# Convolution taps read from PSUM, and scan inputs fetched a step ahead, in a hybrid attention and state-space decoder step

## The chip, the cores and the metric

One core of one Trainium2 chip runs the whole program. The metric is the device time of one execution in microseconds (us). Five engines work side by side, each through its own instruction queue, in order: PE (TensorE, matmuls and transposes), DVE (VectorE), ACT (ScalarE), POOL (GpSimd) and SP (SyncE, which issues the DMAs here). PEld is PE's weight load. Results of PE land in PSUM, everything else is in SBUF or in device memory.

## The reference

One decoder layer for 1024 prompt tokens and 8 sample tokens. A norm feeds one wide projection `h @ w_in`, whose columns go to attention (q, k, v), to the state-space branch (z, xBC, dt) and to two gates. The change lies in the state-space branch:

```python
def _causal_conv(xbc, buf, w, bias):
    xp = jnp.concatenate([buf, xbc], axis=1)
    y = bias + xp[:, 0:L] * w[0]
    for t in range(1, D_CONV):          # D_CONV = 4
        y = y + xp[:, t:t + L] * w[t]
    return jax.nn.silu(y), xp[:, L:]
...
def _ssd(x, dt, A, Bm, Cm, h0):         # chunks of 128 tokens
    lmat = jnp.exp(_segsum(a))
    cb = jnp.einsum('bclgn,bcsgn->bcgls', Cc, Bc)
    y_diag = jnp.einsum('bcgels,bcsgep->bclgep', cb[:, :, :, None] * lmat, xf)
    decay_states = jnp.exp(a_cs[..., -1:] - a_cs)
    states = jnp.einsum('bclgn,bclgep->bcgepn', Bc, xf * decay_states[..., None])
    ...                                 # carry the states from chunk to chunk
    y_off = jnp.einsum('bclgn,bcgepn->bclgep', Cc, new_states[:, :-1]) * jnp.exp(a_cs)[...]
```

`xf` is x times dt. For the prompt `buf` is zero; for a sample token it is the stored window of three earlier tokens, and one step of the recurrence is done on a stored state. The convolution has 4096 channels: 2048 of x, 1024 of B, 1024 of C. There are 8 groups, each with 4 heads (256 channels of x) and 128 channels each of B and C.

## The kernel before

Features lie on partitions, tokens on columns. The 1032 tokens are cut into three chunks of 384, 384 and 264 columns (256 of the prompt and the 8 sample tokens). A `Dense` job computes 128 output features: for each chunk 24 matmuls (8 row tiles, three products of split weights and split inputs, L139 to L141) into one PSUM buffer `mm`, of which there are three, and then `evac` empties it. I call one such chunk a **dense step**. A weight tile comes by DMA (`wraw`), is rounded on ACT (`whi`, `shi`, L96), and POOL takes the rest (`wlo`, `slo`, L97).

The scan stage goes through the 8 groups. For group g the dense jobs are two of z (`z_jobs`, 6 steps) and then the four convolution jobs of group g+1 (`x_jobs`, 12 steps: two of x, one of B, one of C). Between the steps `pump` puts in **side work** of group g from three generators of `ssd_sides`: `chunks` (the scan over 8 chunks of 128 tokens: `prep`, `state`, `out`), `finish_` (norm, then `project`, eight tiles of output features of three chunks each, into the same `mm` buffers), and `decode` (the sample tokens). PE's order is the order in which the code runs; a scheduler sets the order of the other engines, which then work in that order.

What an `x_jobs` step does after its matmuls (L768 to L795): ACT copies PSUM to `rw`, a buffer of 387 columns of which there are two, whose first three columns are the last three of the chunk before (DVE, L775); ACT makes the fourth tap with the bias from PSUM into `acc` (a `ck` tile, L779); DVE adds the three earlier taps, reading `rw` (L781); for the sample tokens three small taps from `cvs` (L785); then tanh (ACT `th`, L789) and the product (DVE, L790). The last columns of a job are an output as well: `tail(i - 1)` is called in the first step of the next job, where PE transposes 11 columns of the `rw` of the step before (L801), and DVE copies them out (L802).

`prep(c)` (L860 to L889) starts the DMAs of the decay rows `ar` (256 KB, two buffers) and `er` where it uses them; ACT turns `ar` into exp(min(0, ...)) (L870, L872); PE transposes x and B and multiplies B with C into one PSUM tile; DVE masks that (`cb`) and makes `xd`; ACT copies `bt` and makes `xw` = `xd` times decay in four instructions (L887); POOL multiplies `ar` by `cb` (L888). `state` multiplies `xw` and `bt` (L894); `out` uses `ar` (L913). `decode` (L822 to L856) sends B and C of the sample tokens through memory (`bc_d`) and loads them broadcast (`bc`, one buffer) at the top of each of its four turns, with the states `hst` (two buffers).

Of the kernel before, what the change touches and what calls it, by code (L numbers as in the profile page):

```python
# [16 lines left out]
D = 1024  # L17
# [23 lines left out]
def _trunk(ctx, tc, nc, I, O):  # L41
# [16 lines left out]
    def h_tiles():  # L58
        return tuple([[hp_.tile([128, nt], F32R, name=p, tag=f"{p}{ci}", bufs=8) for ci, (_, nt) in enumerate(CH)]
                      for _ in range(8)] for p in ('hh', 'hl'))  # L60
# [22 lines left out]
    def load_w(src, r0, kt, c0, n, side=False, into=None, raw=None):  # L83
        """weights of kt row tiles by n columns, split into two float32r parts"""
# [15 lines left out]
    class Dense:  # L100
        """out^T[n features, tokens] for one tile of weight columns"""
        def __init__(self, src, r0, c0, n, x, evac, pre=None):
            self.a = (src, r0, c0, n, x, evac, pre)
            self.units = self.raw = None
# [19 lines left out]
        def steps(self):  # L124
            src, r0, c0, n, x, evac, pre = self.a
            if pre:
                pre()
            xh, xl = x if isinstance(x, tuple) else x()
            nk = len(xh)
            for ci, (t0, nt) in enumerate(CH):  # L130
                idle = 0
                while gated[0] and live[ci // 2] >= CKB[ci // 2] - 1 and idle < 20:
                    clock[0] += 1
                    idle = 0 if pump(2) else idle + 1
                ps = ps_mm()
                for k in range(nk):
                    wh, wl = self.units[k]
                    a, b = xh[k][ci], xl[k][ci]
                    T.matmul(ps[:n, :nt], wh, a, start=(k == 0), stop=False)  # L139
                    T.matmul(ps[:n, :nt], wh, b, start=False, stop=False)  # L140
                    T.matmul(ps[:n, :nt], wl, a, start=False, stop=(k == nk - 1))  # L141
                evac(ci, t0, nt, ps)
                yield
# [11 lines left out]
    def pump(n):  # L155
        """n slots of the side work; the oldest that need not wait come first"""
# [21 lines left out]
    def run(jobs, pace=0.0, after=None, ahead=1):  # L178
        """the dense jobs in order, with pace slots of side work after each step"""
# [40 lines left out]
    h_ = h_tiles()  # L220
    hh, hl = h_

    def rsqrt_cols(y, v, t):
        """y = v ** -0.5: a first guess from the exponent bits, then Newton steps"""
# [6 lines left out]
    class Mod:  # L231
        """512 of the modulation's columns; the weights move"""
# [48 lines left out]
    def rstd_cols(sq, scale, eps, pool):  # L281
        """(scale * column sums + eps) ** -0.5 of 384 columns, as [128, 3]"""
# [17 lines left out]
    with tc.tile_pool(name="p0", bufs=1) as p0:  # L300
# [55 lines left out]
        def make_h(ci):  # L356
# [12 lines left out]
            for k in range(8):  # L369
# [9 lines left out]
                V.tensor_copy(hh[k][ci], h[:, :nt])  # L379
                (P if k % 2 else V).tensor_tensor(hl[k][ci], h[:, :nt], hh[k][ci], op=OP.subtract)  # L380

# [40 lines left out]
    def attn_jobs(u, tiles):  # L422
        """q, k, v of two heads: the prompt's tokens ordered by residue, then the sample tokens"""
# [29 lines left out]
    def attn_side(u, tiles):  # L453
# [22 lines left out]
        def tok(j):  # L476
            # token-major k (where it is an output) and v
# [69 lines left out]
        for j in range(11):  # L547
# [3 lines left out]
            if j == 0:  # L551
                # rows of the sample tokens
# [100 lines left out]
    def dt_side(dp):  # L653
# [46 lines left out]
        A.activation(df, df, AF.Exp)  # L700
        A.activation(cdk.rearrange("p c h -> p (c h)"), p2[:, :256], AF.Exp)
# [11 lines left out]
        # sample: dt, exp(dt A) and D per (head, channel) partition  # L713
# [37 lines left out]
    def x_jobs(gi, tl):  # L751
# [3 lines left out]
        def post():  # L755
            for lo, n, i0, i1 in ((chans[0], 256, 0, 2), (chans[2], 128, 2, 3), (chans[3], 128, 3, 4)):
                src = st['t'][:, i0:i1, :].rearrange("r a b -> r (a b)")
                dma(cpr[:, lo:lo + n], src[0:3])
                dma(dap(O['conv_sample'], 2 * 4096 + lo, [[3 * 4096, 8], [1, n]]), src[3:11])

        jobs = []
        for i, ch in enumerate(chans):
            f = ch // 128
            prev = []
            tl['x'].append([None] * 3)

            def evac(ci, t0, nt, ps, i=i, f=f, prev=prev):
# [15 lines left out]
                if nt > n:  # L783
                    for k in range(3):
                        V.scalar_tensor_tensor(acc[:, n:nt], cvs[:, f, k, :], w[k], acc[:, n:nt],  # L785
                                               op0=OP.mult, op1=OP.add)
                    tl['tail'].append((i, rw, n, nt))
# [5 lines left out]
                if ci == 0 and i > 0:  # L793
                    tail(i - 1)

            def tail(i):
                _, rw, n, nt = tl['tail'][i]
                if i == 0:
                    st['t'] = sa.tile([24, 4, 128], F32, name="tail", tag="tail", bufs=1)
                pt = ps_()  # L800
                T.transpose(pt[:11, :128], rw[:, n:3 + nt], ident)  # L801
                V.tensor_copy(st['t'][:11, i, :], pt[:11, :128])  # L802

            if i == 3:
                def fin(tail=tail):
                    tail(3)
                    post()
                tl['fin'] = fin
            col = (X_C + gi * 256 + i * 128) if i < 2 else ((B_C if i == 2 else C_C) + gi * 128)
            jobs.append(Dense(w_in, 0, col, 128, h_, evac))  # L810
        return jobs

    def ssd_sides(gi, tl):
# [8 lines left out]
        def decode():  # L822
# [5 lines left out]
            rb = sd.tile([8, 2, 128], F32, name="rb", tag="rb", bufs=1)  # L828
# [4 lines left out]
            dma(bc_d[gi].rearrange("k b n -> b k n"), rb)  # L833
            yield from rest(2)
            for bh in range(4):
                bc = sd.tile([128, 2, 2, 128], F32, name="bc", tag="bc", bufs=1)
                dma(bc, dap(bc_d, gi * 2048 + bh * 256, [[0, 128], [1024, 2], [128, 2], [1, 128]]))
                for t in range(2):
                    r0 = bh * 2 * 262144 + (4 * gi + 2 * t) * 8192
                    hst = sd.tile([128, 2, 128], F32, name="hst", tag="hst", bufs=2)  # L840
                    dma(hst, dap(ws, r0, [[128, 128], [262144, 2], [1, 128]]))
# [4 lines left out]
                    tmp = sd.tile([128, 2, 128], F32, name="tmp", tag="tmp", bufs=1)  # L846
                    for i in range(2):
                        A.mul(tmp[:, i, :], bc[:, 0, i, :], dx[:, i:i + 1])
                        V.scalar_tensor_tensor(hst[:, i, :], hst[:, i, :], ds[:, 8 + 2 * bh + i:9 + 2 * bh + i],
                                               tmp[:, i, :], op0=OP.mult, op1=OP.add)  # L850
# [662 lines left out]
```

## Time and profile before

| what | value |
|---|---|
| three timed runs | 2601.06, 2606.17, 2608.93 us (median 2606.17) |
| profiled execution, span | 2599.9 us (the page gives no other time for it) |
| PE busy | 2413.3 us, 93% of the span |
| PE weight loads | 2278.0 us, 88% |
| DVE, ACT, POOL busy | 1409.6, 976.0, 827.7 us (54%, 38%, 32%) |
| scan stage | about 470 to 1480 us |

Matmuls are pipelined, so that a busy PE is not a PE at its peak. The span lies 6.3 us under the median of the timed runs. In the chain of work that ended last PE has 30% of the span, DVE 2%, and nothing else over 1%. The stage of the last projections (1900 to 2500 us) shows PE busy without a gap; the scan stage does not.

### The profile page before, as it was taken

The numbers are of one execution on the slowest core, as the hardware profiler recorded it, in microseconds if no ns is written. First come the engines' busy times: TensorE is split into PE (matmuls) and PEld (weight loads), VectorE is DVE, ScalarE is ACT, GpSimd is POOL, SyncE is SP. The second block draws the span as 40 slices with busy tenths as digits, with TensorE's granted clock in tenths as the row PEclk, the third lists the DMA queues.
The fourth block names the chain that finished last, engine by engine and source line by source line (L and its number), as shares of the span: only waits on it lengthen the run. The fifth ranks groups of instructions, "written<-read, shape, count | busy, mean of one in ns | idle before, by whom it ended". The sixth has DMA issues, their size and how long they took to land. (4 is left out here: it accounts for less than half of the span.)

```text
span 2599.9 us, 42044 instructions
## 1 busy us (share of the span) xinstructions
PE 2413.3 (93%) x15342; PEld 2278.0 (88%) x15342; DVE 1409.6 (54%) x3738; ACT 976.0 (38%) x2476; POOL 827.7 (32%) x759
## 2 busy tenths in 40 slices
PE   6999999988989898989898999889999999999998
PEld 3788888978888888889888898879999999999997
DVE  7634334586777777777778533553733333333336
ACT  6244443454535353535353422242412212221222
POOL 5322222243434343434343333353222122222230
PEclk8999999999999999999999999999999999999999
DMA  6433334243233333333333223332145444511111
GB/s 221 124 89 108 107 92 114 78 107 94 73 88 75 87 73 85 78 82 78 84 80 82 76 64 85 96 117 65 54 164 168 138 154 144 173 45 50 57 41 66
DMA packets 341944, 250.59 MB, mean 96 GB/s; under 512 B 22750, under 2 KB 324393, under 8 KB 339034
## 3 DMA queue, kind: packets, MB, share of 16 engines
q1 hardware_dynamic: 341738, 247.91, 33.4%
q8 instruction: 121, 1.98, 0.3%
q14 instruction: 85, 0.70, 0.1%
HBM read 224.50 MB, written 67.58 MB: 112 GB/s over the span
## 5 line engine op out<-in xcount | busy, mean ns | idle before, releaser
L139 PE MATMUL mm<-hh,whi 128*128 128x384 f32 (+2 forms) x2856 | 939.3, 329 | 2.9 <-ACT whi L96 2.0
L140 PE MATMUL mm<-hl,whi 128*128 128x384 f32 (+2 forms) x2856 | 919.9, 322 | 4.2 <-POOL hl L380 3.6
L141 PE MATMUL mm<-hh,wlo 128*128 128x384 f32 (+2 forms) x2856 | 918.9, 322 | 1.3 <-POOL wlo L97 1.3
L97 POOL TENSOR_TENSOR wlo<-wraw,whi 128x512 fp32r<-128x512 f32 (+2 forms) x304 | 399.0, 1319 | 863.7 <-ACT whi L96 800.0
L139 PEld LDWEIGHTS mm<-hh,whi 128*128 128x128 f32 (+1 forms) x2856 | 546.0, 191 | 12.0 <-issue 3.2
L140 PEld LDWEIGHTS mm<-hl,whi 128*128 128x128 f32 (+1 forms) x2856 | 545.8, 191 | 9.8 <-POOL hl L380 5.9
L141 PEld LDWEIGHTS mm<-hh,wlo 128*128 128x128 f32 (+1 forms) x2856 | 544.4, 191 | 2.7 <-POOL wlo L97 1.7
L96 ACT CAST whi<-wraw 128x512 fp32r<-128x512 f32 (+2 forms) x304 | 182.8, 611 | 358.5 <-PE mm L140 314.3
L1190 DVE SCALAR_TENSOR_TENSOR acc<-mm,mod,acc 128x384 f32<-128x384 f32 (+1 forms) x216 | 123.5, 572 | 244.9 <-PE mm L141 244.9
L140 PE MATMUL mm<-dl,whi 128*128 128x384 f32 (+1 forms) x696 | 223.2, 321 | 0.0
L141 PE MATMUL mm<-dh,wlo 128*128 128x384 f32 (+1 forms) x696 | 222.4, 320 | 0.0
L139 PE MATMUL mm<-dh,whi 128*128 128x384 f32 (+1 forms) x696 | 222.3, 319 | 0.0
L781 DVE SCALAR_TENSOR_TENSOR ck<-rw,cwT,ck 128x384 f32<-128x384 f32 (+1 forms) x288 | 193.1, 671 | 9.2 <-ACT ck L779 7.1
L1303 DVE TENSOR_TENSOR r<-r 128x384 f32<-128x384 f32 (+1 forms) x96 | 69.5, 724 | 185.6 <-ACT r L1302 185.4
L888 POOL TENSOR_TENSOR ar<-ar,cb 128x512 f32<-128x512 f32 x64 | 81.9, 1281 | 245.9 <-ACT ar L872 223.3
L969 PE MATMUL mm<-ck,shi 128*128 128x384 f32 (+1 forms) x384 | 131.2, 342 | 28.2 <-DVE acc L975 13.2
L971 PE MATMUL mm<-ck,slo 128*128 128x384 f32 (+1 forms) x384 | 128.2, 334 | 5.4 <-POOL slo L97 5.4
L139 PEld LDWEIGHTS mm<-dh,whi 128*128 128x128 f32 x696 | 131.1, 188 | 0.0
L140 PEld LDWEIGHTS mm<-dl,whi 128*128 128x128 f32 x696 | 131.0, 188 | 0.0
L141 PEld LDWEIGHTS mm<-dh,wlo 128*128 128x128 f32 x696 | 130.8, 188 | 0.0
L970 PE MATMUL mm<-ck,shi 128*128 128x384 f32 (+1 forms) x384 | 127.5, 332 | 1.3 <-POOL ck L952 1.3
L870 ACT ACTIVATE ar<-ar,acs 128x128 f32<-128x128 f32 x256 | 84.2, 390 | 104.9 <-DMA ar<-ac_d 101.7
(337 smaller groups left out, 3776.4 us busy)
## 6 DMA issues: line engine op xcount, KB each, us to landing
wraw<-w_in SPq DMA_DIRECT2D x164, 256.0 KB
kv_g_sample<-cache_kv_g SPq DMA_DIRECT2D x144, 256.0 KB
wraw<-w_ada SPq DMA_DIRECT2D x96, 256.0 KB
ar<-ac_d SPq DMA_DIRECT2D x64, 256.0 KB
wraw<-w_up SPq DMA_DIRECT2D x64, 256.0 KB
wraw<-w_down SPq DMA_DIRECT2D x58, 256.0 KB
hst<-state_ssm SPq DMA_DIRECT2D x64, 128.0 KB
bc<-bc_d SPq DMA_DIRECT2D x32, 256.0 KB
```

What stands on the lines that cost most here:

```text
L96: A.copy(hi, raw)
L97: P.tensor_tensor(lo, raw, hi, op=OP.subtract)
L139: T.matmul(ps[:n, :nt], wh, a, start=(k == 0), stop=False)
L140: T.matmul(ps[:n, :nt], wh, b, start=False, stop=False)
L141: T.matmul(ps[:n, :nt], wl, a, start=False, stop=(k == nk - 1))
L781: V.scalar_tensor_tensor(acc[:, :n], rw[:, k:k + n], w[k], acc[:, :n], op0=OP.mult, op1=OP.add)
L870: A.activation(ar[:, h, :], ar[:, h, :], AF.Relu, bias=acs[:, c, 4 * gi + h:4 * gi + h + 1], scale=-1.0)
L888: P.tensor_tensor(ar, ar, cb[:, None, :].to_broadcast([128, 4, 128]), op=OP.mult)
L969: T.matmul(ps[:, :nt], hi[:, t, :], a, start=(t == 0), stop=False)
L970: T.matmul(ps[:, :nt], hi[:, t, :], b, start=False, stop=False)
L971: T.matmul(ps[:, :nt], lo[:, t, :], a, start=False, stop=(t == 1))
L1190: V.scalar_tensor_tensor(x[:, t0:t0 + n], ps[:, :n], gate[:, 0:1], x[:, t0:t0 + n], op0=OP.mult, op1=OP.add)
```

## The change

- The inputs `hh` and `hl` of chunks 1 and 2 are laid out with four more columns in front (`HALO`), which repeat the last four tokens of the chunk before. 32 small ACT copies fill them in the stage of the first norm (behind L380 of the kernel before). The four convolution jobs of each group use these wider inputs, so that their PSUM buffer holds the tokens that the taps need; all other jobs use the slices without them.
- `rw`, the PSUM copy and the 3-column copy go. The three taps on DVE read PSUM, with `acc` from SBUF. For the sample tokens bias and three earlier taps are added up once at the stage's start (`conv_side`), and one small instruction per job is left. ACT copies the 11 last columns of each job to `last`, and `fin` transposes all four jobs' columns in one place.
- `ar` is fetched by `load` three chunks ahead (three buffers); `bc` and `hst` one turn ahead (two and three buffers); `tmp` has three small buffers in place of one large.
- `xw` is made by one DVE instruction from PSUM with dt and decay multiplied beforehand, in place of four on ACT; `cb` comes after it and has one buffer; the ACT work on `ar` comes after these in the code.
- The rounded copy `hi_` in `norm` moves from DVE to ACT.

```diff
+                m = nt + (self.halo if ci else 0)
                 for k in range(nk):
                     wh, wl = self.units[k]
                     a, b = xh[k][ci], xl[k][ci]
-                    T.matmul(ps[:n, :nt], wh, a, start=(k == 0), stop=False)
+                    T.matmul(ps[:n, :m], wh, a, start=(k == 0), stop=False)
...
+                if ci:
+                    for x, y in zip(hx_, h_):
+                        A.copy(x[k][ci][:, :HALO], y[k][ci - 1][:, CH[ci - 1][1] - HALO:])
...
+        V.tensor_tensor(dcy, dcy, dtk[:, :8], op=OP.mult)
...
+        def fin():
+
+            pt = ps_()
+            for i in range(4):
+                T.transpose(pt[:11, i * 128:(i + 1) * 128], st['last'][:, i, :], ident)
+            for p, parts in enumerate((((chans[0], 0, 256),), ((chans[2], 0, 128), (chans[3], 128, 128)))):
+                t = sa.tile([11, 256], F32, name="tail", tag="tail", bufs=2)
+                A.copy(t, pt[:11, p * 256:(p + 1) * 256])
...
-            def evac(ci, t0, nt, ps, i=i, f=f, prev=prev):
+            def evac(ci, t0, nt, ps, i=i, f=f):
...
-                rw = sa.tile([128, 387], F32, name="rw", tag="rw", bufs=2)
-                if ci == 0:
-                    V.memset(rw[:, 0:3], 0.0)
-                else:
-                    V.tensor_copy(rw[:, 0:3], prev[-1][:, 384:387])
-                prev.append(rw)
-                A.copy(rw[:, 3:3 + nt], ps[:, :nt])
+                x0 = HALO if ci else 0
                 acc = ck(nt, 1)
-                A.activation(acc[:, :nt], ps[:, :nt], AF.Identity, bias=bias, scale=w[3])
+                A.activation(acc[:, :n], ps[:, x0:x0 + n], AF.Identity, bias=bias, scale=w[3])
                 for k in range(3):
-                    V.scalar_tensor_tensor(acc[:, :n], rw[:, k:k + n], w[k], acc[:, :n],
+                    d = 3 - k
+                    o = 0 if ci else d
+                    V.scalar_tensor_tensor(acc[:, o:n], ps[:, x0 + o - d:x0 + n - d], w[k], acc[:, o:n],
                                            op0=OP.mult, op1=OP.add)
                 if nt > n:
...
+                    A.copy(st['last'][:, i, :], ps[:, x0 + n - 3:x0 + nt])
...
-                if ci == 0 and i > 0:
-                    tail(i - 1)
...
-            jobs.append(Dense(w_in, 0, col, 128, h_, evac))
+            jobs.append(Dense(w_in, 0, col, 128, hx_, evac, halo=HALO))
...
+            load(0)
             yield from rest(2)
             for bh in range(4):
-                bc = sd.tile([128, 2, 2, 128], F32, name="bc", tag="bc", bufs=1)
-                dma(bc, dap(bc_d, gi * 2048 + bh * 256, [[0, 128], [1024, 2], [128, 2], [1, 128]]))
...
+                load(bh + 1)
+                bc, hs_ = got[bh]
...
+        def load(c):
+
+            if c > 7:
+                return
+            ar = D_[c] = sd.tile([128, 4, 128], F32, name="ar", tag="ar", bufs=3)
+            dma(ar, dap(ac_d, 4 * gi * 1024 + c * 128, [[0, 128], [1024, 4], [1, 128]]))
...
         def prep(c):
-            ar = sd.tile([128, 4, 128], F32, name="ar", tag="ar", bufs=2)
-            dma(ar, dap(ac_d, 4 * gi * 1024 + c * 128, [[0, 128], [1024, 4], [1, 128]]))
+            ar = D_.pop(c)
...
             A.copy(bt, pt[:, 256:384])
+            V.tensor_tensor(xw, pt[:, :256].rearrange("p (h d) -> p h d", h=4),
+                            dcy[:, c, hs, None].to_broadcast([128, 4, 64]), op=OP.mult)
+            V.tensor_tensor(cb, pt[:, 384:512], tri, op=OP.mult)
             for h in range(4):
-                A.mul(xw[:, h, :], xd[:, h, :], dcy[:, c, 4 * gi + h:4 * gi + h + 1])
...
-                V.tensor_copy(hi_[t, ci], y)
+                A.copy(hi_[t, ci], y)
...
                 if c + 2 < 8:
                     prep(c + 2)
+                load(c + 3)
```

On PE, in the convolution of the sixth group, behind the first step of the last job, before (`L801` is the transpose of `rw`, `L944` one of the norm's; the next dense step begins behind it):

```order
L140 MATMUL mm<-hl,whi 128x384
L141 MATMUL mm<-hh,wlo 128x384
L801 MATMUL ps<-cst,rw 11x128
L944 MATMUL ps<-cst,rstd 128x128 x3
L139 MATMUL mm<-hh,whi 128x384
```

And now, in the same place:

```order
L142 MATMUL mm<-hh,whi 128x384
L143 MATMUL mm<-hl,whi 128x384
L144 MATMUL mm<-hh,wlo 128x384
L960 MATMUL ps<-cst,rstd 128x128 x3
L142 MATMUL mm<-hh,whi 128x388
```

The transpose has left the convolution's steps. Four of them stand together in the next group's first step of z, behind the transposes of `prep`, where the fourth job's stood before.

On ACT, from the second to the third step of the third convolution job of that group, before (`rw` is the copy of PSUM, `ck<-mm` the fourth tap, `th` the tanh):

```order
L789 ACTIVATE th<-ck 128x384
L777 COPY rw<-mm 128x384
L779 ACTIVATE ck<-mm,vecT,cwT 128x384
L932 ACTIVATE sq<-ck 128x264
L96 CAST whi<-wraw 128x512 x2
L789 ACTIVATE th<-ck 128x384
L777 COPY rw<-mm 128x264
L779 ACTIVATE ck<-mm,vecT,cwT 128x264
L96 CAST shi<-wraw 128x256
L789 ACTIVATE th<-ck 128x264
```

And now:

```order
L801 ACTIVATE th<-ck 128x384
L788 ACTIVATE ck<-mm,vecT,cwT 128x384
L948 ACTIVATE sq<-ck 128x264
L97 CAST whi<-wraw 128x512 x2
L801 ACTIVATE th<-ck 128x384
L788 ACTIVATE ck<-mm,vecT,cwT 128x256
L799 COPY last<-mm 128x11
L801 ACTIVATE th<-ck 128x264
L97 CAST shi<-wraw 128x256
```

The copies of PSUM are gone and the small `last` copy stands in front of the tanh of its step; the tanh of one step still stands ahead of the fourth tap of the next.

On SP, the DMAs behind the store of B and C of the sample tokens in that stage, before (`bc` is their broadcast load, `wraw` weights):

```order
L833 DMA bc_d<-rb 8x2x128
L80 DMA wraw<-w_o_ssd 128x2x128
L837 DMA bc<-bc_d 128x2x256
L80 DMA wraw<-w_o_ssd 128x2x128
L862 DMA ar<-ac_d 128x4x128
L853 DMA ssm_sample<-hst 128x2x128
```

And now:

```order
L829 DMA bc_d<-rb 8x2x128
L81 DMA wraw<-w_o_ssd 128x2x128
L836 DMA bc<-bc_d 128x2x256 x2
L875 DMA ar<-ac_d 128x4x128
L81 DMA wraw<-w_o_ssd 128x2x128 x2
L861 DMA ssm_sample<-hst 128x2x128
```

The second turn's `bc` moved up behind the first; the first still stands close behind the store that it reads.

## Rows read from the trace of the kernel before

**Rows 1.** Stretches: us; busy us (count) of PE, PEld, DVE, ACT, POOL; clock; DMA; GB/s

```profile
470.00:1480.00 1010.00, 906.46 (x5876) 859.92 (x5876) 739.63 (x2067) 472.76 (x1323) 378.53 (x360) 0.96 0.33 83
1900.00:2500.00 600.00, 600.00 (x3827) 600.00 (x3826) 203.76 (x431) 131.76 (x258) 137.91 (x107) 1.00 0.35 112
```

**Rows 2.** Waits of PE in 470 to 1480 us: total us, times, longest us

```profile
PE ps L801 <- ACT rw L777: 40.5, 15, 4.7
PE ps L894 <- ACT xw L887: 21.2, 13, 3.5
PE mm L969 <- ACT shi L96: 12.5, 6, 2.6
PE mm L969 <- DVE acc L975: 11.1, 9, 2.2
PE mm L971 <- POOL slo L97: 5.4, 6, 0.9
```

**Rows 3.** PE's timeline in the sixth group: start us, us, instruction, [idle before <-releaser]

```profile
1101.61 0.34 PE L141 MATMUL mm<-hh,wlo 128*128 128x384 f32 x1
...
1114.38 0.39 PE L801 MATMUL ps<-cst,rw 128*11 128x128 f32 x1 [4.67 <-ACT rw L777]
```

**Rows 4.** ACT's timeline in the same steps

```profile
1071.28 0.40 ACT L870 ACTIVATE ar<-ar,acs 128x128 f32<-128x128 f32 x1 [4.85 <-DMA ar<-ac_d]
...
1087.08 0.99 ACT L870 ACTIVATE ar<-ar,acs 128x128 f32<-128x128 f32 x3 [3.53 <-DMA ar<-ac_d]
...
1113.53 0.52 ACT L789 ACTIVATE th<-ck 128x384 f32<-128x384 f32 x1 [3.67 <-DVE rstd L227]
1113.96 0.36 ACT L777 COPY rw<-mm 128x264 f32<-128x264 f32 x1
```

**Rows 5.** DVE's timeline just before that

```profile
1108.88 0.16 DVE L229 SCALAR_TENSOR_TENSOR rstd<-rstd 128x3 f32<-128x3 f32 x1
...
1109.69 1.22 DVE L228 SCALAR_TENSOR_TENSOR rstd<-rstd 128x3 f32<-128x3 f32 x1
...
1111.18 1.61 DVE L781 SCALAR_TENSOR_TENSOR ck<-rw,cwT,ck 128x384 f32<-128x384 f32 x1
...
1112.82 0.62 DVE L781 SCALAR_TENSOR_TENSOR ck<-rw,cwT,ck 128x384 f32<-128x384 f32 x1
```

**Rows 6.** POOL's timeline at the same time

```profile
1109.48 2.89 POOL L97 TENSOR_TENSOR wlo<-wraw,whi 128x512 fp32r<-128x512 f32 x2 [7.88 <-DMA conv_sample<-tail]
```

**Rows 7.** Waits of ACT in 470 to 1480 us

```profile
ACT ar L870 <- DMA ar<-ac_d: 101.7, 40, 5.3
ACT tmp L848 <- DMA bc<-bc_d: 87.3, 27, 5.8
```

**Rows 8.** Groups by form in 470 to 1480 us: count | busy us, mean ns | idle before

```profile
L139 PE MATMUL mm<-hh,whi 128*128 128x384 f32 x753 | 266.7, 354 | 0.0
...
L781 DVE SCALAR_TENSOR_TENSOR ck<-rw,cwT,ck 128x384 f32<-128x384 f32 x179 | 133.5, 746 | 6.6 <-ACT ck L779 4.5
...
L139 PE MATMUL mm<-hh,whi 128*128 128x264 f32 x376 | 110.5, 294 | 0.0
...
L887 ACT ACTIVATE xw<-xd,dcy 128x64 f32<-128x64 f32 x256 | 71.4, 338 | 0.0
...
L781 DVE SCALAR_TENSOR_TENSOR ck<-rw,cwT,ck 128x256 f32<-128x256 f32 x90 | 48.8, 542 | 2.0 <-ACT ck L779 2.0
...
L883 DVE TENSOR_TENSOR xd<-ps,dtk 128x256 f32<-128x256 f32 x64 | 26.2, 410 | 0.0
...
L775 DVE COPY rw<-rw 128x3 f32<-128x3 f32 x59 | 21.9, 371 | 25.4 <-ACT rw L777 25.3
```

**Rows 9.** Min/median/max ns of the taps (470 to 1480) and L1190 (1900 to 2500)

```profile
L781 DVE SCALAR_TENSOR_TENSOR ck<-rw,cwT,ck x269: 462/605/1676, 469.8 to 1393.3; 128x384 f32<-128x384 f32 x90, 128x256 f32<-128x256 f32 x45
L1190 DVE SCALAR_TENSOR_TENSOR acc<-mm,mod,acc x168: 482/617/621, 1902.8 to 2488.2; 128x384 f32<-128x384 f32 x112, 128x256 f32<-128x256 f32 x56
```

**Rows 10.** The stage in which the halo is filled, as rows 1

```profile
70.00:80.00 10.00, 7.98 (x48) 4.88 (x48) 8.64 (x30) 4.80 (x9) 4.80 (x6) 0.98 0.01 2
```

More of the change, by code (lines that the diff above doesn't have):

```diff
@@ L56, in ps_, with h_tiles @@
         return psum.tile([128, 512], F32, name="ps", tag="ps", bufs=5)
-    def h_tiles():
-        return tuple([[hp_.tile([128, nt], F32R, name=p, tag=f"{p}{ci}", bufs=8) for ci, (_, nt) in enumerate(CH)]
-                      for _ in range(8)] for p in ('hh', 'hl'))
+    def h_tiles(halo=0):
+        return tuple([[hp_.tile([128, nt + (halo if ci else 0)], F32R, name=p, tag=f"{p}{ci}", bufs=8)
+                       for ci, (_, nt) in enumerate(CH)] for _ in range(8)] for p in ('hh', 'hl'))
     def chs(t):
@@ L218, in _trunk @@
     ac_d = dram.tile([2, 32, 1024], F32, name="ac_d")
-    h_ = h_tiles()
-    hh, hl = h_
+    HALO = 4
+    hx_ = h_tiles(HALO)
+    hh, hl = hx_
+    h_ = tuple([[t[:, HALO if ci else 0:] for ci, t in enumerate(r)] for r in x] for x in hx_)
     def rsqrt_cols(y, v, t):
@@ L833, in decode, with load @@
             dma(bc_d[gi].rearrange("k b n -> b k n"), rb)
+            got = {}
+            def load(bh):
+                if bh > 3:
+                    return
+                bc = sd.tile([128, 2, 2, 128], F32, name="bc", tag="bc", bufs=2)
+                dma(bc, dap(bc_d, gi * 2048 + bh * 256, [[0, 128], [1024, 2], [128, 2], [1, 128]]))
+                hs_ = []
+                for t in range(2):
+                    r0 = bh * 2 * 262144 + (4 * gi + 2 * t) * 8192
+                    hst = sd.tile([128, 2, 128], F32, name="hst", tag="hst", bufs=3)
+                    dma(hst, dap(ws, r0, [[128, 128], [262144, 2], [1, 128]]))
+                    hs_.append((r0, hst))
+                got[bh] = bc, hs_
+            load(0)
             yield from rest(2)
             for bh in range(4):
-                bc = sd.tile([128, 2, 2, 128], F32, name="bc", tag="bc", bufs=1)
-                dma(bc, dap(bc_d, gi * 2048 + bh * 256, [[0, 128], [1024, 2], [128, 2], [1, 128]]))
[L838 to L841, printed above, removed]
+                load(bh + 1)
+                bc, hs_ = got[bh]
+                for t, (r0, hst) in enumerate(hs_):
                     ds = dsel[:, 2 * gi + t, :]
@@ L845, in decode @@
                     V.tensor_tensor(dx[:, :2], xcol, ds[:, 2 * bh:2 * bh + 2], op=OP.mult)
-                    tmp = sd.tile([128, 2, 128], F32, name="tmp", tag="tmp", bufs=1)
                     for i in range(2):
-                        A.mul(tmp[:, i, :], bc[:, 0, i, :], dx[:, i:i + 1])
+                        tmp = sd.tile([128, 128], F32, name="tmp", tag="tmp", bufs=3)
+                        A.mul(tmp, bc[:, 0, i, :], dx[:, i:i + 1])
                         V.scalar_tensor_tensor(hst[:, i, :], hst[:, i, :], ds[:, 8 + 2 * bh + i:9 + 2 * bh + i],
-                                               tmp[:, i, :], op0=OP.mult, op1=OP.add)
-                        V.tensor_tensor_reduce(tmp[:, i, :], hst[:, i, :], bc[:, 1, i, :], 1.0, 0.0,
+                                               tmp, op0=OP.mult, op1=OP.add)
+                        V.tensor_tensor_reduce(tmp, hst[:, i, :], bc[:, 1, i, :], 1.0, 0.0,
                                                OP.mult, OP.add, dx[:, 4 + i:5 + i])
@@ L980, in chunks @@
         def chunks():
+            while gi and tls[gi - 1]['c'] < 8:
+                yield 'wait'
+            for c in range(3):
+                load(c)
             while tl['nx'] < 12:
@@ L1028, in finish @@
             assert idle < 50
-    tls = [dict(z=[], x=[], tail=[], nz=0, nx=0, c=0, dec=0) for _ in range(8)]
+    tls = [dict(z=[], x=[], nz=0, nx=0, c=0, dec=0) for _ in range(8)]
     atl = [[] for _ in range(6)]
@@ L1055, in _trunk @@
     sa = sa_cm.__enter__()
-    cvs = sa.tile([128, 32, 3, 8], F32, name="cvs")
+    cvs = sa.tile([128, 32, 8], F32, name="cvs")
     def conv_side():
@@ L1072, in conv_side @@
                             ident[:24, :24])
-            V.tensor_copy(cvs[:, f0:f0 + 16], ps[:, :384].rearrange("p (i b k) -> p i k b", i=16, k=3))
+            pv = ps[:, :384].rearrange("p (i b k) -> p i k b", i=16, k=3)
+            fs = slice(f0, f0 + 16)
+            c, t = (sa.tile([128, 384], F32, name="th", tag="th", bufs=2)[:, :128]
+                    .rearrange("p (i b) -> p i b", i=16) for _ in range(2))
+            for k in range(3):
+                V.tensor_tensor(t if k else c, pv[:, :, k, :], cwT[:, k, fs, None].to_broadcast([128, 16, 8]),
+                                op=OP.mult)
+                if k:
+                    V.tensor_tensor(c, c, t, op=OP.add)
+            V.tensor_tensor(cvs[:, fs], c, vecT[:, R_CB + f0:R_CB + f0 + 16, None].to_broadcast([128, 16, 8]),
+                            op=OP.add)
             yield
```

55 lines of the change are left out of this document (21 added, 34 removed).

## The prediction

> **What bounds the kernel now.** I first read the busy time by stretch. From 1900 to 2500 us PE is busy for 600.0 of 600 us at a granted clock of 1.00; from 470 to 1480 us, the scan stage, for 906 of 1010 at a mean clock of 0.96 [rows 1]. The stages differ in what ends the waits, so I then read PE's own waits in the scan stage [rows 2], and from the longest of them back to its cause [rows 3 to 6]. The other engines are not full there (DVE 740 us, ACT 473, POOL 379 of 1010, [rows 1]); what counts is how late they are, since each works its queue in order.
>
> The longest wait of PE is that of the small transpose L801 for the copy `rw`: 40.5 us in 15 places [rows 2]. One of them: PE stands for 4.67 us up to 1114.38, so from 1109.71, since ACT makes `rw` only at 1113.96 [rows 3, 4]. ACT stood 3.67 us in front of a tanh, for the taps that end on DVE at 1113.4 [rows 4, 5]. And DVE was late for two reasons. ACT had itself stood 4.85 and 3.53 us in this group for a DMA of the decay rows [rows 4]; and two of DVE's instructions took 1.22 and 1.61 us in place of some 0.16 and 0.61, while POOL worked on two weight tiles [rows 5, 6]. Over the stage ACT stood 101.7 us for the decay rows and 87.3 us for `bc` [rows 7].
>
> [...]
>
> **The change part by part**, against the profiled execution, whose span is 2599.9 us; the median of the timed runs is 6.3 us above it.
>
> *The transposes of `rw`.* All of the 40.5 us go, because no transpose stands in the convolution any more. The four that stand together later take the place of the fourth job's, 8 in all; where the fourth job's transposes did not wait, and the `last` copies are in ACT's queue ahead of the tanh. −40.5 (bounds −24, if the eight waited 2 us each, and −40.5).
>
> *`xw`.* PE waits 21.2 us in 13 places for ACT's four `xw` instructions [rows 2], which take 4 x 0.338 us behind the four on `ar` and their exponent [rows 8]. One DVE instruction takes their place; its nearest row is `xd` from the same PSUM tile, 410 ns [rows 8]. It needs no decay rows. `bt` remains on ACT. −17 (bounds −10 and −21).
>
> *Prefetch.* `project` waits 12.5 us for ACT's `shi`, 5.4 us for POOL's `slo` that follows it, and 11.1 us for DVE's `acc` [rows 2], 29 in all. ACT's queue holds `tmp` and `ar` ahead of `shi`, and stands on their DMAs [rows 7]; DVE's `hst` stands on `tmp`. A chunk's decay rows are now issued one chunk earlier, some 6 us, where the worst wait was 5.3 us [rows 7]; so that wait should all but vanish. `bc` of turns 2 to 4 comes a turn earlier, but that of turn 1 still stands close behind the store that it reads, so one of four of these waits remains. I take 60%: −17.5 (bounds 0 and −29).
>
> *The clock.* 75 of the 91 us of PE's waits above go. I take 60% of the 40 us: −24 (bounds 0 and −40).
>
> *The halo's columns.* 32 jobs x 2 chunks x 24 matmuls = 1536 matmuls with 4 more columns. A matmul of 384 columns has a mean of 354 ns, one of 264 of 294 ns [rows 8]: 0.5 ns a column, 2.0 ns for four, +3.1 us. All of it lies on PE.
>
> *The halo's copies.* 32 on ACT, each at most the 338 ns of an instruction with 64 columns [rows 8], 11 us at most. In that stage ACT is busy for 4.8 of 10 us and PE for 8.0 [rows 10], so most lies in ACT's idle time. +2 (bounds 0 and +11).
>
> *The taps, and who holds PSUM.* Before, an `mm` buffer came free with the copy and the fourth tap, both on ACT. Now it is held until the third tap is done on DVE (and, in the last chunk, the `last` copy), and the step three later waits for that. Behind a waiting step on PE stands all of PE's work. An instruction of that form (PSUM times a column, plus SBUF) is L1190: 482 and 617 ns for 256 and 384 columns, with a maximum of 621. The taps from `rw` have a median of 605 but a maximum of 1676 [rows 9] and means of 746 and 542 [rows 8]. So 179 taps become 129 ns shorter and 90 become 60 ns shorter: −28 us on DVE. The copies of 3 columns (21.9 us [rows 8]) go as well; `xw` brings 64 x 0.410 = 26 us. DVE is a little lighter by that alone, ACT by the 71 us of `xw` [rows 8] and the copies. How late are the taps now? In the example the taps that end at 1113.4 are those of the step that ended at 1101.95 [rows 3], 11.5 us earlier. The step three later would have started at about 1110, just behind 1109.71, so that PE would have stood 3.4 us for PSUM in place of 4.67 for `rw`. Of these 11.5 us, 8.4 come from the two DMA waits above [rows 4], which go, and about 2 from the two long DVE instructions, of which the tap's can't recur by [rows 9]. I take +1 us a group for what is left: +8 (bounds 0 and +27, 3.4 us in each of 8 groups).
>
> *The rest* (three small sums for the sample tokens, rounding on ACT, the dt product, once) lies beside PE's dense steps, on engines with 270 us and more to spare [rows 1]: 0; without that cover it would cost a few us.
>
> [...] L1190, from PSUM, takes 617 ns at 384 columns, and the tap from SBUF 605 in the median [rows 9]: 12 ns apart. [...] Here the rows have both forms, 12 ns apart, and the long ones on the SBUF side alone; the sum goes by them.
>
> **The sum.** −40.5 −17 −17.5 −24 = −99; +3.1 +2 +8 = +13.1; together −85.9. 2599.9 − 85.9 = 2514.0; with 6.3 above the span, **2520 us**.
>
> **The rivals.**
>
> *Half of it (2560 us).* The wait for `rw` turns into one for `mm`: DVE and ACT stay in step with each other, as tanh still waits for the taps and the next fourth tap stands behind that tanh. For: the order on ACT shows just that chain. Price: 3.4 us in each group, 27 in place of 8; and with these gaps 17 of the clock's 24 and 5 of the prefetch's 17.5 stay away: 2520 + 19 + 17 + 5 = 2561. Against: the main cause of the lateness, the DMA waits, goes. The prefetch could be to blame as well: `hst` of the next turn needs the buffer of a store, and SP, which holds `wraw` of `project` behind it, would stand.
>
> *Slower (2675 us).* One mechanism: DVE, busy for 740 of 1010 us [rows 1], is the real limit of the convolution, and PSUM now ties PE to it. With the lateness of today, 11.5 us against the 8.1 from 1101.95 to 1110, PE would lose 3.4 us at each of the last six steps of 8 groups: 163 us. With all the other terms: 2520 − 8 + 163 = 2675. It decides from a loss of 1.8 us at each of these 48 steps (86 us). Against: a late step pushes its followers back as well, so they do not add up; and DVE has 270 us free.
>
> *All of it (2480 us).* Every wait of rows 2 and the whole 40 us of the clock return: 40.5 + 21.2 + 29 + 40 = 131, less 5: 2599.9 − 126 + 6.3 = 2480.
>
> *It doesn't do what it says.* The scheduler could put the loads no earlier on SP. It has the first `bc` where it was; if the decay rows too came no earlier, the convolution would stay late, and this is the half case.
>
> **How the numbers follow.** Around the sum (2495 to 2540) 0.53; all of it (below 2495) 0.17; half (2540 to 2598) 0.22; no change that can be told from none 0.03; slower 0.05. A difference of 0.3% (8 us) is about what a measurement of this kernel can tell from no change. The range takes in the whole of the sum's band, most of the half case and most of the other: 2475 to 2568. Faster 0.92, same 0.03, slower 0.05.
>
> **What would show it.** Right: no wait of PE for ACT in the convolution; ACT's waits for `ar` near zero and those for `bc` at a quarter; taps of about 0.62 and 0.48 us with no long ones; a mean clock of 0.98 or more between 470 and 1400 us; waits of the dense steps for `mm` under 10 us. Wrong: PE waiting at the start of convolution steps for DVE's taps or the tanh's chain, and DVE busy without a gap; `wraw` late behind `hst` on SP; or other waits of `project` in place of these.

## The result, and the profile after

| kernel | median, us | ratio to before, 95% interval |
|---|---|---|
| before (4 runs beside it) | 2603.6 | 1 |
| changed (4 runs, 2537.0 to 2540.4) | 2538.1 | 0.9746 (0.9730 to 0.9762) |

The changed kernel is 65 us faster, with a span of 2537.4 us against 2599.9. The prediction said 2520, with a range of 2475 to 2568: the sign and the range hold, and the gain is 18 us smaller than the sum had it. The experiments show that the largest term of the sum came out at its size for a wrong cause, that another failed, and that the gain could have been nearly twice as large.

Stretches of the changed kernel, with the columns of [rows 1]; its last projections begin some 60 us earlier:

```profile
470.00:1420.00 950.00, 894.38 (x5899) 847.30 (x5899) 655.09 (x1916) 412.61 (x1071) 367.58 (x360) 0.99 0.34 89
1840.00:2440.00 600.00, 600.00 (x3820) 600.00 (x3819) 204.21 (x430) 131.21 (x256) 137.75 (x107) 1.00 0.35 110
```

In the scan stage PE stands idle for 56 of 950 us, where it was 104 of 1010 [rows 1], and the clock is at 0.99 in place of 0.96. The last projections are as before: all of the gain lies in the scan. PE's waits there (470 to 1480 us, as for all waits below; total us, times, longest), as [rows 2]:

```profile
PE mm L985 <- DVE acc L991: 22.4, 27, 3.1
PE ps L929 <- POOL ar L904: 10.0, 5, 2.5
PE ps L960 <- DVE rstd L234: 7.8, 8, 2.7
PE mm L142 <- DVE ck L792: 5.0, 7, 1.0
PE ps L925 <- DVE state L916: 4.1, 3, 1.8
...
PE ps L910 <- DVE xw L897: 1.2, 1, 1.2
```

The waits for `rw` (40.5) and ACT's `xw` (21.2) of [rows 2] are gone; what PE waited 11.1 us for, DVE's `acc`, is now 22.4 us, and the lines under it have grown (`L929`, `L960`: 3.5 and 4.9 us before) or are new. `L142 <- DVE ck` is the wait for a PSUM buffer that the taps hold: 5.0 us. ACT's waits in the same stretch, as [rows 7]:

```profile
ACT ar L901 <- DMA ar<-ac_d: 109.8, 40, 6.9
...
ACT tmp L856 <- DMA bc<-bc_d: 36.3, 18, 4.3
```

Those for `bc` fell from 87.3 us to 36.3. Those for the decay rows, loaded three chunks ahead, did not fall at all (101.7 before). The timeline of ACT at the start of the sixth group's convolution tells why (start us, us, instruction, idle before it in brackets):

```profile
1025.52 0.24 ACT L896 COPY bt<-ps 128x128 f32<-128x128 f32 x1
1031.94 1.28 ACT L901 ACTIVATE ar<-ar,acs 128x128 f32<-128x128 f32 x4 [6.17 <-DMA ar<-ac_d]
1033.25 0.63 ACT L903 ACTIVATE ar<-ar 128x512 f32<-128x512 f32 x1
1033.79 0.65 ACT L788 ACTIVATE ck<-mm,vecT,cwT 128x384 f32<-128x384 f32 x1
```

And SP, PE and DVE of the same kernel there:

```profile
1025.79 0.45 SPq L875 DMA_DIRECT2D ar<-ac_d  x1
```

```profile
1027.72 0.34 PE L144 MATMUL mm<-hh,wlo 128*128 128x384 f32 x1
```

```profile
1034.48 0.61 DVE L792 SCALAR_TENSOR_TENSOR ck<-mm,cwT,ck 128x381 f32<-128x381 f32 x1 [5.45 <-ACT ck L788]
```

SP issues the load at 1025.79, and it lands 6.2 us later. ACT, whose order a scheduler sets, has the relu on these rows as its next instruction and stands for the whole of the 6.2 us, though the rows are for a chunk still to come. The first convolution step ended on PE at 1028.06; its fourth tap stands behind the relu in ACT's queue and starts at 1033.79, and DVE is idle for 5.45 us for it. The load came earlier, its first use came earlier by as much.

### The profile page after: what moved, and what is told of

Its sections match the earlier page's. It is cut to its first block, busy times and chain, and to the rows that moved or that the text cites. A ratio compares the mean times of both kernels' runs of the same rounds, so it can differ in the third digit from the quotient of the medians.

```text
span 2537.4 us, 41601 instructions
## 1 busy us (share of the span) xinstructions
PE 2398.7 (95%) x15342; PEld 2263.9 (89%) x15342; DVE 1319.3 (52%) x3573; ACT 917.9 (36%) x2252; POOL 817.0 (32%) x759
## 5 line engine op out<-in xcount | busy, mean ns | idle before, releaser
L142 PE MATMUL mm<-hh,whi 128*128 128x384 f32 (+4 forms) x2856 | 938.4, 329 | 7.9 <-DVE ck L792 5.0
L143 PE MATMUL mm<-hl,whi 128*128 128x384 f32 (+4 forms) x2856 | 919.7, 322 | 4.0 <-POOL hl L385 3.0
L144 PE MATMUL mm<-hh,wlo 128*128 128x384 f32 (+4 forms) x2856 | 920.0, 322 | 1.0 <-POOL wlo L98 1.0
L142 PEld LDWEIGHTS mm<-hh,whi 128*128 128x128 f32 (+1 forms) x2856 | 542.2, 190 | 18.3 <-ACT whi L97 7.9
L142 PE MATMUL mm<-dh,whi 128*128 128x384 f32 (+1 forms) x696 | 222.3, 319 | 0.0
L792 DVE SCALAR_TENSOR_TENSOR ck<-mm,cwT,ck 128x384 f32<-128x384 f32 (+4 forms) x288 | 163.6, 568 | 69.7 <-ACT ck L788 65.9
L985 PE MATMUL mm<-ck,shi 128*128 128x384 f32 (+1 forms) x384 | 130.0, 339 | 25.3 <-DVE acc L991 22.4
L142 PEld LDWEIGHTS mm<-dh,whi 128*128 128x128 f32 x696 | 131.1, 188 | 0.0
L901 ACT ACTIVATE ar<-ar,acs 128x128 f32<-128x128 f32 x256 | 85.3, 391 | 109.9 <-DMA ar<-ac_d 109.8
L986 PE MATMUL mm<-ck,shi 128*128 128x384 f32 (+1 forms) x384 | 123.5, 322 | 1.1 <-POOL ck L968 1.1
```

The source lines that it names most:

```text
L142: T.matmul(ps[:n, :m], wh, a, start=(k == 0), stop=False)
L143: T.matmul(ps[:n, :m], wh, b, start=False, stop=False)
L144: T.matmul(ps[:n, :m], wl, a, start=False, stop=(k == nk - 1))
L792: V.scalar_tensor_tensor(acc[:, o:n], ps[:, x0 + o - d:x0 + n - d], w[k], acc[:, o:n], op0=OP.mult, op1=OP.add)
L901: A.activation(ar[:, h, :], ar[:, h, :], AF.Relu, bias=acs[:, c, 4 * gi + h:4 * gi + h + 1], scale=-1.0)
L985: T.matmul(ps[:, :nt], hi[:, t, :], a, start=(t == 0), stop=False)
```

## The experiments

Each kernel was timed beside the kernel before (2603 to 2606 us), with four runs or more of its own.

| kernel | us | ratio to before, 95% interval |
|---|---|---|
| conv_alone | 2561.3 | 0.9839 (0.9819 to 0.9858) |
| conv_alone_copy | 2607.0 | 1.0006 (0.9997 to 1.0016) |
| no_ahead | 2535.9 | 0.9744 (0.9728 to 0.9760) |
| xw_act | 2526.6 | 0.9707 (0.9689 to 0.9725) |
| ar_late | 2490.8 | 0.9566 (0.9547 to 0.9584) |
| before_late | 2607.2 | 1.0006 (0.9996 to 1.0017) |
| late_no_ahead | 2546.6 | 0.9770 (0.9755 to 0.9784) |
| late_no_dec | 2509.8 | 0.9631 (0.9617 to 0.9646) |
| late_xw_act | 2508.3 | 0.9623 (0.9609 to 0.9638) |
| late_na_copy | 2601.8 | 0.9981 (0.9969 to 0.9993) |
| dec_thin | 2542.3 | 0.9754 (0.9738 to 0.9770) |
| best | 2483.4 | 0.9534 (0.9520 to 0.9548) |

### The convolution part alone, and what in it gains

**conv_alone** is the kernel before with the halo, the PSUM taps, the `last` copies, `fin` and the summed sample rows, and with nothing else of the diff.

> The kernel before with the convolution part of the change alone: halo columns and their copies, taps from PSUM, the small `last` copies and `fin`, the summed rows of the sample tokens. Decay rows, B, C and states are fetched as before, `xw` stays on ACT and the rounded copy on DVE. Parts add up: the 40.5 us of waits for `rw` go, against +3 for the columns, +3 for the copies and about +5 for `mm`, and some 12 us of the clock come back: 2604 - 41 = 2563 us, with `xw` waits near 21 us as before. Rival, tied: without the prefetch ACT and DVE stay late, the wait for `rw` turns into one for `mm` of 25 us or more, and the time is 2590 us or above.

Measured: 2561.3 us. The parts add up here: this part alone gains 42 us, where the whole change gains 65, without any prefetch. ACT's waits for its DMAs are still there:

```profile
ACT ar L865 <- DMA ar<-ac_d: 103.6, 41, 7.0
ACT tmp L843 <- DMA bc<-bc_d: 94.8, 31, 6.0
```

But from which of its parts does the gain come? **conv_alone_copy** puts the copy of PSUM back and lets the taps and the `last` copy read it; no transpose comes back:

```diff
+                rw = sa.tile([128, 388], F32, name="rw", tag="rw", bufs=2)
+                A.copy(rw[:, :x0 + nt], ps[:, :x0 + nt])
                 for k in range(3):
...
-                    V.scalar_tensor_tensor(acc[:, o:n], ps[:, x0 + o - d:x0 + n - d], w[k], acc[:, o:n],
+                    V.scalar_tensor_tensor(acc[:, o:n], rw[:, x0 + o - d:x0 + n - d], w[k], acc[:, o:n],
...
```

> The kernel before with the convolution part alone (2561 us), where each step's PSUM tile is copied to SBUF by ACT again and the taps and the small `last` copy read that copy: no transposes in the convolution, but taps from SBUF. Theory, the gain of the convolution part is the taps' length: the taps are long again beside POOL (mean of 384 columns above 0.74 us), PE's waits move to other instructions behind the late DVE, and the time is 2590 us or above, most of the way back to 2604. Rival, it is the transposes of `rw` on PE, as predicted: these stay away, and the time is 2575 us or below.

Measured: 2607.0 us, so that the whole gain of the part is lost again (the halo's columns and copies, some 7 us by the sizes measured below, are in this time). The prediction's step, that the transposes' leaving gives the 40.5 us, falls. PE's waits of conv_alone_copy show where these went:

```profile
PE ps L941 <- DVE rstd L234: 34.4, 10, 4.5
PE ps L891 <- ACT xw L884: 21.1, 14, 2.7
```

L941 are the norm's small transposes, which stood right behind L801 in PE's order. PE has to pass them next, their `rstd` comes from the same late DVE, and they wait 34.4 us (9.4 in conv_alone) where L801 had waited 40.5. The two kernels differ in two things, ACT's copies and the place from which the taps read, and no run parts them. The trace speaks for the second. DVE does not stand longer for ACT in front of its taps (conv_alone, then conv_alone_copy):

```profile
DVE ck L791 <- ACT ck L787: 37.0, 24, 5.8
```

```profile
DVE ck L793 <- ACT rw L789: 37.4, 45, 5.6
```

But the taps themselves take longer, 192 us in all in place of 153. Their min/median/max in ns (470 to 1400 us), in the same order:

```profile
L791 DVE SCALAR_TENSOR_TENSOR ck<-mm,cwT,ck x271: 469/608/620, 469.6 to 1355.6; 128x256 f32<-128x256 f32 x46, 128x384 f32<-128x384 f32 x45, 128x382 f32<-128x382 f32 x15, 128x381 f32<-128x381 f32 x15
```

```profile
L793 DVE SCALAR_TENSOR_TENSOR ck<-rw,cwT,ck x270: 464/611/1672, 471.0 to 1396.1; 128x384 f32<-128x384 f32 x45, 128x256 f32<-128x256 f32 x45, 128x381 f32<-128x381 f32 x15, 128x383 f32<-128x383 f32 x15
```

The medians are 3 ns apart, the maxima 1052. DVE and POOL of conv_alone_copy in the seventh group:

```profile
1255.11 0.61 DVE L793 SCALAR_TENSOR_TENSOR ck<-rw,cwT,ck 128x382 f32<-128x382 f32 x1
...
1255.90 1.37 DVE L793 SCALAR_TENSOR_TENSOR ck<-rw,cwT,ck 128x383 f32<-128x383 f32 x1
...
1258.92 3.82 DVE L793 SCALAR_TENSOR_TENSOR ck<-rw,cwT,ck 128x384 f32<-128x384 f32 x3 [0.37 <-ACT rw L789]
```

```profile
1255.27 2.87 POOL L949 TENSOR_TENSOR ck<-ck 128x384 fp32r<-128x384 f32 x2 [1.29 <-DVE ck L948]
1259.47 2.85 POOL L98 TENSOR_TENSOR wlo<-wraw,whi 128x512 fp32r<-128x512 f32 x2 [1.33 <-PE mm L144]
```

A tap that starts while POOL subtracts two SBUF tiles takes 1.37 us. Of the three in the last row of DVE, which take 3.82 together, the first starts ahead of POOL's `wlo` and takes 0.62; the other two take 1.60 and 1.53. Counted over the scan by overlap with POOL's busy spans: in conv_alone_copy 43 of 270 taps took over 0.8 us, all 43 beside POOL; in the kernel before 39 of 268, all 39 beside POOL; in conv_alone and the changed kernel none, though 126 and 148 of 270 lay beside POOL. Of the 43, 41 start while a POOL instruction runs, and they end 0.28 to 0.42 us behind the end of that instruction, as if such a tap stood until POOL was done. So taps with two SBUF tensors lengthen here, and those with one tensor from PSUM don't.

**late_na_copy** made the same test in another kernel, late_no_ahead below (2546.6 us):

> To be compared with the kernel with ACT's work behind `bt` and without the prefetch (run beside it): each convolution step's PSUM tile is first copied to SBUF by ACT, and the taps and the small `last` copy read that copy, as in the kernel before; halo columns, `fin` and all else stay. Theory, holding PSUM costs next to nothing and the copy is only more work: ACT has 96 instructions (40 us) more, some taps take over 1 us beside POOL's work on SBUF, and the time is 5 to 15 us longer. Rival, PSUM held through the taps and the dearer PSUM reads cost: it is 5 us or more shorter. Between them, nothing: within 5 us.

Measured: 2601.8 us, 55 us longer. The sign is the first theory's, its size some four times too small. Here too DVE stands no longer for ACT in front of the taps (36.2 us against 35.9), while the taps take 202 us in place of 152 and ACT's tanh waits 200.5 us for them in place of 82.2. That the price is DVE's lateness, and not ACT's time for the copies, is read from these waits and was not run by itself.

### Decay rows: fetched early, used late

**no_ahead** puts all loads back where they were (`load(c)` in `prep`, two `ar` buffers; `load(bh)` at the top of its turn, one `bc` and two `hst` buffers).

> The changed kernel with the prefetch undone: decay rows are loaded in the chunk's own preparation (two buffers), B, C and states at the top of their own turn (one and two buffers). Parts add up: PE's waits in project go back from 23 to about 32 us and a little of the clock goes: 2538 + 14 = 2552 us. Rival, no use: since ACT stands for the decay rows as long as before (110 us against 102), the earlier loads buy nothing and the time stays within 4 us of 2538. Rival, tied: the convolution is early only because of the prefetch; without it PE waits 25 us or more for `mm` and the time is 2570 us or above.

Measured: 2535.9 us. No use: the prefetch as written gains nothing, and the convolution is early without it. **ar_late** adds one edge of order to the changed kernel:

```diff
-            A.copy(bt, pt[:, 256:384])
+            bti = A.copy(bt, pt[:, 256:384])
...
+            with tc.issue_after(bti.ins):
-            for h in range(4):
-                A.activation(ar[:, h, :], ar[:, h, :], AF.Relu, bias=acs[:, c, 4 * gi + h:4 * gi + h + 1],
+                for h in range(4):
+                    A.activation(ar[:, h, :], ar[:, h, :], AF.Relu, bias=acs[:, c, 4 * gi + h:4 * gi + h + 1],
...
```

> The changed kernel with one order added: ACT's work on the decay rows is queued behind the copy `bt` of the same chunk, so that it can't be put right behind the load. Theory, early use costs nothing on PE: ACT's waits for the decay rows fall from 110 us to under 30, PE's waits in project for ACT and POOL stay under 4 us, and the time stays within 5 us of 2538. Rival, the early use is itself the gain: the exponents come late for POOL's product, PE's waits for POOL grow from 10 us to 25 or more and the time is 2550 us or above. Rival, the waits on ACT still cost: the time falls to 2530 us or below.

Measured: 2490.8 us, 47 us less than the changed kernel. The third reading holds: ACT's waits did cost. The same place in ACT's timeline of ar_late:

```profile
997.10 0.27 ACT L896 COPY bt<-ps 128x128 f32<-128x128 f32 x1 [1.02 <-DVE xd L894]
997.26 1.28 ACT L902 ACTIVATE ar<-ar,acs 128x128 f32<-128x128 f32 x4
998.58 0.63 ACT L904 ACTIVATE ar<-ar 128x512 f32<-128x512 f32 x1
1000.71 0.67 ACT L788 ACTIVATE ck<-mm,vecT,cwT 128x384 f32<-128x384 f32 x1 [1.50 <-PE mm L144]
```

The rows have landed when ACT comes to them (in the whole scan ACT has no wait for them left, where it was 109.8 us), and here ACT waits for PE at the fourth tap. Its scan stage, and PE's three longest waits there:

```profile
470.00:1420.00 950.00, 930.92 (x6226) 893.69 (x6225) 663.81 (x1962) 434.35 (x1104) 390.72 (x383) 0.99 0.36 93
```

```profile
PE mm L986 <- DVE acc L992: 11.3, 16, 2.1
PE ps L961 <- DVE rstd L234: 4.3, 1, 4.3
PE ps L652 <- DVE uT L647: 2.8, 2, 1.8
```

PE is idle for 19 of 950 us where it was 56; its wait for POOL's product is 0.5 us in place of 10.0. **before_late** makes the same edge in the kernel before, **late_no_ahead** in the changed kernel without the prefetch, and **late_no_dec** takes away the prefetch of B, C and states alone.

> The kernel before with one thing changed: ACT's work on the decay rows of a chunk is queued behind the copy `bt` of that chunk, so that it can't be put right behind the load. Theory, ACT's early standing is a cost of its own in either kernel: ACT's waits for the decay rows fall from 102 us to under 30, PE's wait for `rw` from 40 us to about 20, and the time is 2604 - 35 = 2569 us or below. Rival, it pays only with the rest of the change: `xw`, still on ACT, now comes behind the late exponent, PE's waits for it grow from 21 us to 40 or more, and the time stays within 8 us of 2604 or rises.

> The changed kernel with ACT's work on the decay rows behind `bt` (2491 us), and the prefetch of decay rows, B, C and states undone. Theory, the prefetch pays once its rows are not used at once: without it ACT stands for B and C some 110 us and for the decay rows 30 us or more, and the time is 2491 + 15 = 2506 us or above. Rival, the order alone is the gain: within 5 us of 2491.

> The changed kernel with ACT's work on the decay rows behind `bt` (2491 us), with the prefetch of B, C and states alone undone; the decay rows are still loaded three chunks ahead. Without both prefetches it was 2547 us. Theory, the decay rows' prefetch carries the larger part: 2491 + 20 = 2511 us or below, ACT's waits for decay rows stay under 10 us and those for B and C are about 100. Rival, B, C and states carry it, since ACT stands for them in front of the casts of project: 2530 us or above.

Measured: 2607.2, 2546.6 and 2509.8 us. The order alone gives nothing in the kernel before. The reason that the rival named, `xw`, was not it, since that wait stayed at 21.6 us; ACT still stood for the rows:

```profile
ACT ar L884 <- DMA ar<-ac_d: 65.7, 27, 4.1
```

The four corners of the changed kernel:

| | relu where the scheduler puts it | relu behind `bt` |
|---|---|---|
| loads as before | 2535.9 | 2546.6 |
| loads ahead | 2538.1 | 2490.8 |

Neither edit alone gains; both together gain 45 us. Without the prefetch the late relu still stands for a load issued too late (rows of late_no_ahead):

```profile
ACT tmp L855 <- DMA bc<-bc_d: 104.2, 29, 6.7
ACT ar L902 <- DMA ar<-ac_d: 84.9, 29, 4.7
```

Of the prefetch's 56 us in the right-hand column, 19 go when B, C and states are no longer fetched ahead (2509.8 less 2490.8), and another 37 when the decay rows aren't either.

### `xw`, and the limit of project

**xw_act** makes `xw` on ACT again, behind the work on `ar`, so that DVE's `cb` has no `xw` ahead of it; **late_xw_act** does the same with the relu behind `bt`.

> The changed kernel with `xw` back on ACT in four instructions from `xd` (the product of dt and decay is left out again, `cb` comes before the ACT work as before). Parts add up: the waits of the state matmul for ACT's `xw` come back with some 20 us, PE's waits for POOL's product with `cb` (10 us) fall to about 4: 2538 + 15 = 2553 us. Rival, hidden: with the decay rows worked on early, ACT is free when `xd` is ready, the wait is under 8 us and the time is within 4 us of 2538.

> The changed kernel with ACT's work on the decay rows behind `bt` (2491 us), and with `xw` back on ACT, behind that work. Theory, `xw` on ACT gained 12 us only since it put the decay rows' work later: with the order set apart, that gain is gone, PE waits for ACT's `xw` 10 us or more and the time is 2491 + 12 = 2503 us. Rival, DVE is the limit of project: with 64 DVE instructions of 0.41 us (26 us) less, PE's waits for DVE's `acc` fall from 11 us to under 6 and the time is 2483 us or below.

Measured: 2526.6 us, 12 less than the changed kernel, below both theories; and 2508.3 us, 17 more than ar_late. Its first theory had the sign and 5 us less, but not by the wait that grew (PE waited 1.9 us for `xw`, and 21.0 for `acc` in place of 11.3). PE's wait for `xw` in xw_act, and that for `acc` in late_xw_act:

```profile
PE ps L909 <- ACT xw L902: 4.0, 4, 2.7
```

```profile
PE mm L985 <- DVE acc L991: 21.0, 20, 3.6
```

So moving `xw` to DVE is worth 17 us where ACT does not stand for the decay rows, and costs 12 where it does. Nor is that move what took PE's 21.2 us of waits for `xw` [rows 2] away: with `xw` on ACT they are 4.0 us. In xw_act ACT's waits for decay rows are 76 us in place of 110 and PE's for POOL's product 3.3 in place of 10.0; whether the earlier `cb` brings this was not run by itself.

The 23 us between conv_alone and the changed kernel thus belong to no single part that was run: to undo the prefetch or `xw` makes the changed kernel no slower. Neither the later place of ACT's work on `ar` in `prep` nor the rounded copy on ACT was run by itself.

**dec_thin** asks whether DVE has become the limit of project, where PE now waits 22.4 us for `acc`.

> The changed kernel without the sum over states in the decode step (128 DVE instructions of 0.34 us, 43 us in all, are left out, so that the sample tokens' part is not computed fully). Theory, DVE is the limit of project now: PE's waits for DVE's `acc` fall from 20 us to under 9 and the time is 2538 - 13 = 2525 us or below. Rival, `acc` is late since DVE itself stands for ACT and ACT for its DMAs: the waits stay at 15 us or more and the time is within 5 us of 2538.

Measured: 2542.3 us, with these waits of PE:

```profile
PE mm L983 <- DVE acc L989: 12.8, 15, 2.3
PE ps L927 <- POOL ar L902: 10.0, 5, 2.5
PE mm L983 <- ACT tmp L856: 7.9, 5, 1.8
PE ps L958 <- DVE rstd L234: 7.8, 8, 1.5
PE mm L983 <- DVE dx L853: 5.7, 5, 1.3
```

The wait for `acc` fell by 10 us, and 13.6 us of waits of the same line for `tmp` and `dx` took its place: 26.4 us on L983 against 22.4. So 43 us less of DVE's work gave no time, and DVE's load is not the limit there. In ar_late, with all of DVE's work, the wait for `acc` is 11.3.

### A version that beats both

**best** is ar_late with the 32 halo copies ordered behind ACT's last work of the first norm.

> The changed kernel with ACT's work on the decay rows behind `bt` (2491 us), and the 32 small halo copies put behind ACT's last work of the first norm. Theory, the 3 us that the stage of the dt job lost to them come back: 2488 us. Rival, the 6 us of copies only move in front of the next job's weights: 2491 us or above.

Measured: 2483.4 us, 4.7% under the kernel before. The stage from the dt job's first matmul to that of attention takes 29.2 us, as before the change, where the changed kernel took 32.2 and ar_late 32.0. These 3 us are the copies'; the other 4 lie in small differences of stages that the edit does not touch, and their cause was not looked for.

## Why the prediction was right, and where not

- **The transposes of `rw`, −40.5.** The wait went, and about that much time (conv_alone: 42 us in all). The size was luck, since the cause was wrong: with the transposes away and the taps on SBUF nothing is gained. PE then waits for the late engine at what it must pass next (34.4 us at the norm's transposes). I had put 8.4 of the 11.5 us of lateness down to ACT's DMA waits and 2 to DVE's long instructions [rows 4, 5]; conv_alone kept the DMA waits (104 and 95 us) and still gained 42 us. The term of the taps, which I had at 28 us of DVE's time and at none on the path, is the one that carries it, as far as the traces of the two copies show.
- **`xw`, −17.** The wait fell from 21.2 to 1.2 us, and the DVE instruction takes 0.419 us against 0.410 predicted. But with `xw` on ACT the wait is 4.0 us as well, and what the move is worth hangs on the rest: 17 us in ar_late, −12 in the changed kernel.
- **Prefetch, −17.5.** This step failed. Undone, it changes the time by 2 us. The step from "A chunk's decay rows are now issued one chunk earlier" to "so that wait should all but vanish" took the first use to stay where it was; the scheduler moved it with the load, and the wait is 109.8 us. The rival that the change doesn't do what it says looked at SP's order alone, where the loads did come earlier. Waits for `bc` fell to 42%, not to a quarter. In project the waits for `shi` and `slo` vanished, that for `acc` doubled: 29 us became some 23.
- **The clock, −24.** 0.96 of 1010 us [rows 1] is 40 us lost, 0.99 of 950 some 10: about −30. The sum's 60% of the 40 was an estimate that no run shows; three quarters went. The scan had 82 us of stretches at a granted clock of 0.50 before, in which matmuls of 384 columns start 320 ns apart in place of 173 (medians), 20 after, and 14 in ar_late.
- **Halo columns, +3.1.** From the triple of matmuls at 1024.60 to that at 1027.72 six triples of 384 columns take 3.12 us; from 1030.42 to 1034.12 seven of 388 take 3.70:

```profile
1024.60 0.33 PE L144 MATMUL mm<-hh,wlo 128*128 128x384 f32 x1
...
1030.42 0.34 PE L144 MATMUL mm<-hh,wlo 128*128 128x388 f32 x1
...
1034.12 0.34 PE L144 MATMUL mm<-hh,wlo 128*128 128x388 f32 x1
```

  A triple grows from 0.520 to 0.529 us, 2.9 ns a matmul, or 4.4 us if all 1536 grow by as much.
- **Halo copies, +2.** +3.0. Each is 0.19 us, not the 0.34 of the bound, but they stand in ACT's queue between the instructions that make the stage's `h`; behind them, in best, they cost nothing that shows.
- **Taps that hold PSUM, +8.** 5.0 us, none longer than 1.0. The half case and the slower case, which both rest on this wait, did not come.
- **Not in the sum:** PE's waits for POOL's product (3.5 to 10.0 us), for `rstd` (4.9 to 7.8) and for the state sum on DVE (4.1, new).

The misses partly cancel. The sum had a span of 2514.0 us, and 2537.4 was measured: 23 us more. Of these about 11 are the prefetch in project and 13 the waits that were not in the sum, against −7 from the clock and −4 from the other terms together; the remaining 10 are not accounted for. The median lies 0.7 us above the span and not 6.3, which takes 6 us off again and leaves the 18. That 2538 lies so far inside the range is in part luck.

To copy a matmul's output to SBUF first, ahead of the three taps that read it, does not pay in this kernel: the two copies made it 46 and 55 us slower. Nor do the 12 ns that the prediction has between the two forms [rows 9] show in the taps themselves: their medians are 608 ns from PSUM (conv_alone) and 611 from SBUF (conv_alone_copy).

## What to carry to other kernels

In this kernel a load that was moved ahead gained only once its first use stayed where it was: where a scheduler orders the engine, tie the use to an instruction near its need, and look in the trace for the engine that stands just behind the issue. A wait on PE names the place and not always the cause: before a term is put on removing the instruction that waits, ask what the next instruction would wait for, and take away the lateness itself. Edits that help one late engine need not add up (in the four corners one edit alone cost 2 us, the other 11, and both together gained 45): test them in pairs.

## What the runs showed of the hardware

The size of one effect was not expected: DVE's taps with both tensors in SBUF take up to 1.67 us in place of 0.61 beside POOL's work on SBUF, and with one of the two in PSUM never more than 0.62, in the 126 and 148 cases that lay beside POOL in conv_alone and the changed kernel. Of the lengthened ones 41 of 43 in conv_alone_copy, and 36 of 39 in the kernel before, end 0.28 to 0.42 us behind the end of the POOL instruction that ran when they started. The final product of the convolution in the changed kernel (L802, both tensors in SBUF) still shows it: 21 of 91 take over 0.8 us, up to 1.60, all beside POOL. One load of the decay rows (256 KB) took 6.2 us from issue to use, longer than a convolution step of 384 columns (eight triples of 0.52 us).
